# A two-layer decoder trunk: hidden blocks ranked earlier, a split cut in two, and the last pair of layer 1 by seven products

## The chip, the cores and the metric

The kernel runs on one core of one Trainium2 chip. The metric is the device time of one execution in microseconds. One profiled execution was taken of the kernel before; its trace has the start and duration of every instruction, what ended each idle time, and the issue and landing of every DMA.

## The reference

Two layers on 256 rows of 1024 numbers. Layer 0 mixes tokens by differential attention, layer 1 by block-sparse attention; each is followed by the MLP, around which this case turns:

```python
def squared_relu_mlp(h, w1, w2):
    return jnp.square(jax.nn.relu(h @ w1)) @ w2      # w1 1024x4096, w2 4096x1024

# for each layer i:
#   x = x + mixer_i(rmsnorm(x, attn_norm[i]))
#   x = x + squared_relu_mlp(rmsnorm(x, mlp_norm[i]), w_ff1[i], w_ff2[i])
# out = rmsnorm(x, final_norm)
```

## The kernel before

**Numbers in halves.** Every matmul operand is kept as two parts, `hi` (a rounded copy) and `lo` (what is left), and a product of two operands is three matmuls: hi·hi, lo·hi and hi·lo.

**Units.** The weights come in 96 units of 1 MB (some in pieces): `load` (L148) issues a unit's DMA on SP into one of four buffers `raw`, `need` calls for loads seven units ahead, and a split makes `hi` and `lo` of it: ACT copies (`hi`), DVE subtracts (`lo = raw − hi`), in `split_part` (L194 to L196). Layer 0 has units 0 to 47, layer 1 units 48 to 95. In layer 0, units 16 and 17 are the first two f1 pairs; from there on f1 unit of pair p is 14+2p and f2 unit of pair q is 19+2q, so that 41, 43, 45, 46, 47 are f2 of pairs 11, 12, 13, 14, 15 and 44 is f1 of pair 15. Layer 1's have 48 more (93, 94, 95: f2 of pairs 13, 14, 15).

There are three kinds of split. Most units go by `split_part`. The f1 units (`split_partly`, L184) do 3 of 8 chunks with ACT and an accumulating DMA of POOL. The f2 units go by `split_sums` (L165): besides `hi` and `lo` of the four 512-wide quarters, it makes three sums of quarters (`ts`, L177; then `raw` itself is changed by L179 and L180) with parts `thi` and `tlo`, which the seven products want. The `hi` of the whole raw (128x2048) waits for L180; only its upper half f=0 (128x1024) is complete after L179. L183 to L196 are where this happens.

**The MLP** (L684 to L922) goes over 16 pairs p of hidden blocks. `f1` (L694) puts a pair's activations into PSUM by 48 matmuls of 128x256, always in bank 0 (except p = 1); `hidden(p)` (L710) takes them out by relu and square on ACT (L717, L718), makes four sums on DVE (L722 to L724: `g`, 8 blocks in all) and splits them into `gh` and `gl`. `f2(p, ...)` (L732) multiplies by w2 with seven products in place of eight (as Strassen does for 2x2 blocks): seven PSUM banks M1 to M7 of 128x512, 3 matmuls each, 21 per pair. f2 runs two pairs behind f1. The last pair (15) goes by `direct` (L749), plain products of 24 matmuls that are put on top of the banks whose sums are ready or into a bank of its own, `rest`. `m_out` and `add` (L759 to L789) put the seven banks together into the rows xs: M1 is copied to `um` by ACT first, then DVE adds M6, M7, M5, M4, M3 in a chain, and M2.

**Order.** A tile scheduler with priorities orders each engine. Work has the rank of its place in the program; splits have a rank 150 places behind (`LATER`), and a block under `high_priority(offset=SOONER)` is ranked 100 places ahead. The PE order of attention (from L591) and the end of layer 1 (from L887) are written out by hand.

Of the kernel before, what the change touches and what calls it, by code (L numbers as in the profile page):

```python
# [9 lines left out]
F32 = mybir.dt.float32  # L10
F32R = mybir.dt.float32r
AF = mybir.ActivationFunctionType
# [3 lines left out]
D = 1024  # L16
T = 256
# [17 lines left out]
def kernel(  # L35
# [61 lines left out]
    for i in range(2):  # L97
# [33 lines left out]
        def f2_unit(j, a):  # L131
            U[i, "f2", j, a] = unit([P, 2, D], [
                ((slice(None),), f2[:, 4 * j + 2 * a: 4 * j + 2 * a + 2, :])])
            units[-1]["how"] = "sums" if (j, a) != (7, 1) else RING

# [29 lines left out]
    def split_sums(u):  # L165
# [15 lines left out]
        split_part(*(k.rearrange("p a b -> p (a b)") for k in (ts, thi[:, 1:], tlo[:, 1:])))  # L181
        split_part(*(k.rearrange("p a b -> p (a b)") for k in (raw, hi, lo)))

# [189 lines left out]
    def mixer(i, parts):  # L373
# [217 lines left out]
        with tc.manual_schedule(engines={mybir.EngineType.PE}):  # L591
# [34 lines left out]
            if i == 0:  # L626
                wo0(0)
                scores(6, 7)
                with tc.high_priority(offset=SOONER):
                    a3(5)  # L630
                wo0(1)
                a4(4)
                wo0(2, 3)
                a4(5)
# [49 lines left out]
    def mlp(i, parts):  # L684
# [4 lines left out]
        nc.vector.reciprocal(r2, v)  # L689
        NP = FF // P // 2  # L690
        Z = {}
        G = {}

        def f1(f, k0, k1):  # L694
# [12 lines left out]
            if f % 2 and k1 == KC:  # L707
                hidden(p)

        def hidden(p):  # L710
# [8 lines left out]
            n = 4  # L719
            if p < NP - 1:  # L720
                tt = nc.vector.tensor_tensor
                tt(g[:, 4], g[:, 1], g[:, 3], op=ALU.add)  # L722
                tt(g[:, 5:7], g[:, 1:5:3], g[:, 0:1].to_broadcast([P, 2, P]), op=ALU.subtract)
                tt(g[:, 7], g[:, 2], g[:, 6], op=ALU.subtract)  # L724
                n = 8
# [5 lines left out]

        def f2(p, ks):  # L732

            need(i, "f2", p // 2, p % 2)
            u = units[U[i, "f2", p // 2, p % 2]]
            gh, gl = G[p]
            for k in ks:
                g, names, w, n = SEVEN[k]
                if type(w) is tuple:
                    hi, lo = (u[q][:, w[0], w[1] * H:w[1] * H + H] for q in names)  # L740
                else:
                    hi, lo = (u[q][:, w] for q in names)
                if p == 0:
                    M[k] = bank(n, f"m{i}_{k}")
                for x, y in ((gh, hi), (gh, lo), (gl, hi)):
                    mm(M[k], x[:, g], y, start=p == 0 and x is gh and y is hi,  # L746
                       stop=p == LAST - 1 and x is gl, skip_group_check=True)

# [42 lines left out]
        def product(k):  # L791
            for p in range(LAST - 2, LAST):
                f2(p, (k,))
# [7 lines left out]
        for p in range(2, NP):  # L801
            f1(2 * p, 0, 8)
            f1(2 * p + 1, 0, 8)
            if p < LAST:
                f2(p - 2, SEVEN)
        if i == 0:
            parts3 = new_parts("e0")
            for p in (LAST - 2, LAST - 1):
                f2(p, (2, 7))
# [23 lines left out]
        else:  # L833
# [39 lines left out]

            for p in (LAST - 2, LAST - 1):
                f2(p, (5, 7))
# [4 lines left out]
            m_out(5)  # L880
            rest = bank(0, "rest")
            direct(1, H, D, rest, opens=True)
            add(1, 1, rest)
            product(4)
            direct(1, 0, H, M[4])
            m_out(4)
            with tc.manual_schedule():  # L887
                product(3)
                direct(0, H, D, M[3])
                y_sq(1, 512, 1024, 0)  # L890
# [6 lines left out]
                m_out(3)  # L897
                product(2)
                direct(0, 0, T, M[2][:, :T])
                scale_act(1, 512, 1024, r1)  # L900
# [8 lines left out]
                tail = bank(1, "tail")[:, :T]  # L909
                direct(0, T, H, tail, opens=True)  # L910
                y_add(0, 256, 512, tail)
# [48 lines left out]
```

## Time and profile before

| | us |
|---|---|
| three runs | 584.31, 584.61, 1980.6 |
| median | 584.61 |
| profiled execution, whole | 584.85 |
| its span (first to last instruction) | 583.0 |
| PE busy | 568.9 |
| DVE busy | 477.2 |
| ACT busy | 395.7 |

The span is what the trace shows; 1.85 us of the profiled execution lie around it. Engines are PE (matmul), PEld (its weight loads, which overlap), DVE, ACT, POOL and SP (which issues the loads of weights). PE's granted clock averaged 0.996 over the span. To read the tables: `out<-in` are the program's tiles, `x30` a count, and the idle time before an instruction is followed by what ended it.

### The profile page before, as it was taken

The page shows a single profiled execution, that of the slowest core. Times are in us where ns is not written, and L with a number is a line of the kernel's source. Part 1 is how long each engine was busy: PE and PEld are TensorE (multiplying, and loading weights), DVE is VectorE, ACT ScalarE, POOL GpSimd, SP SyncE. Part 2 cuts the span into 40 slices and gives each one's busy share as a digit, 9 for nine tenths or more (in the row PEclk, how much of TensorE's full clock was granted, in tenths as well). Part 3 has the DMA queues.
Part 4 walks back from the last instruction along what each step waited for, and adds up shares of the span by engine and source line. Part 5 has one row for each costly group of instructions (what it writes and reads, how often), then busy time and mean ns, then how long its engine had stood idle before and what let it go on. Part 6 is the DMA issues. An engine that isn't in the chain of part 4 may idle for free.

```text
span 583.0 us, 9723 instructions
## 1 busy us (share of the span) xinstructions
PE 568.9 (98%) x3784; PEld 509.0 (87%) x3784; DVE 477.2 (82%) x740; ACT 395.7 (68%) x632; POOL 89.2 (15%) x105
## 2 busy tenths in 40 slices
PE   8999999999999999999999999999999999999995
PEld 7889897899989899898789988878989989899874
DVE  4889578399999999988996664646999999998896
ACT  6776376297687786966675655645877686787653
POOL 6011001000011010100030760600001010010003
PEclk9999999999999999999999999999999999999998
DMA  9997444225878979876969445442467878979502
GB/s 304 291 324 237 153 137 144 74 73 194 233 233 247 246 211 247 235 215 217 268 189 264 146 146 158 140 136 70 142 179 241 235 213 249 257 209 293 154 0 73
DMA packets 94718, 113.36 MB, mean 194 GB/s; under 512 B 2480, under 2 KB 77520, under 8 KB 94672
## 3 DMA queue, kind: packets, MB, share of 16 engines
q1 hardware_dynamic: 84752, 103.03, 55.4%
q0 software_dynamic: 9760, 9.45, 10.9%
q8 instruction: 29, 0.48, 0.3%
q10 hardware_dynamic: 160, 0.27, 0.1%
q14 instruction: 17, 0.14, 0.1%
HBM read 111.69 MB, written 1.05 MB: 193 GB/s over the span
## 4 chain that ended last, share of the span: by engine, by line
PE 73%; DVE 14%; ACT 4%; DMA 4%; issue 3%; POOL 1%; SPq 0%; POOLq 0%; DVEq 0%; ACTq 0%
PE m L746 17%; PE f L704 8%; PE f L706 8%; PE f L705 8%; DVE lo L196 6%; PE z L396 4%; PE z L397 4%; PE z L398 4%; DMA raw<-in_w_ff_dram 3%; PE v L417 3%; PE v L419 3%; PE v L418 3%; ACT hi L195 2%; PE wo L552 2%; PE wo L554 2%
## 5 line engine op out<-in xcount | busy, mean ns | idle before, releaser
L195 ACT ACTIVATE hi<-raw 128x1024 fp32r<-128x1024 f32 (+3 forms) x136 | 173.7, 1294 | 105.5 <-DVE raw L180 53.6
L196 DVE TENSOR_TENSOR lo<-raw,hi 128x1024 fp32r<-128x1024 f32 (+3 forms) x134 | 203.4, 1533 | 44.3 <-ACT hi L195 42.5
L191 POOL DMA_DIRECT2D lo<-in_w_ff_dram x24 | 30.8, 1283 | 289.3 <-ACT lo L190 127.1
L704 PE MATMUL f<-xT_(0, 'm')_1444,hi 128*128 128x256 f32 x256 | 71.7, 281 | 0.0
L704 PE MATMUL f<-xT_(1, 'm')_4420,hi 128*128 128x256 f32 x256 | 71.6, 280 | 0.0
L705 PE MATMUL f<-xT_(0, 'm')_1444,hi 128*128 128x256 f32 x256 | 71.4, 280 | 0.0
L705 PE MATMUL f<-xT_(1, 'm')_4420,hi 128*128 128x256 f32 x256 | 71.4, 280 | 0.0
L706 PE MATMUL f<-xT_(1, 'm')_4420,lo 128*128 128x256 f32 x256 | 71.3, 279 | 0.0
L706 PE MATMUL f<-xT_(0, 'm')_1444,lo 128*128 128x256 f32 x256 | 71.3, 279 | 0.0
L704 PEld LDWEIGHTS f<-xT_(0, 'm')_1444,hi 128*128 128x128 f32 x256 | 48.0, 188 | 0.9 <-ACT g L717 0.3
L704 PEld LDWEIGHTS f<-xT_(1, 'm')_4420,hi 128*128 128x128 f32 x256 | 48.0, 188 | 0.8 <-ACT g L717 0.2
L705 PEld LDWEIGHTS f<-xT_(0, 'm')_1444,hi 128*128 128x128 f32 x256 | 47.9, 187 | 0.7
L705 PEld LDWEIGHTS f<-xT_(1, 'm')_4420,hi 128*128 128x128 f32 x256 | 47.9, 187 | 0.7
L706 PEld LDWEIGHTS f<-xT_(1, 'm')_4420,lo 128*128 128x128 f32 x256 | 48.1, 188 | 0.0
L706 PEld LDWEIGHTS f<-xT_(0, 'm')_1444,lo 128*128 128x128 f32 x256 | 48.1, 188 | 0.0
L746 PE MATMUL m<-hi,gl 128*128 128x512 f32 x120 | 47.4, 395 | 0.0
L746 PE MATMUL m<-hi,gh 128*128 128x512 f32 x120 | 47.3, 394 | 0.0
L746 PE MATMUL m<-lo,gh 128*128 128x512 f32 x120 | 47.3, 394 | 0.0
L195 ACT ACTIVATE gh<-g 128x1024 fp32r<-128x1024 f32 (+1 forms) x32 | 32.9, 1028 | 14.8 <-DVE g L724 14.4
L177 DVE TENSOR_TENSOR ts<-raw 128x1024 f32<-128x1024 f32 x30 | 36.6, 1220 | 4.6 <-DMA raw<-in_w_ff_dram 4.6
L746 PE MATMUL m<-thi,gl 128*128 128x512 f32 x90 | 35.8, 398 | 2.5 <-DVE gl L196 2.5
L196 DVE TENSOR_TENSOR gl<-g,gh 128x1024 fp32r<-128x1024 f32 (+1 forms) x32 | 37.8, 1186 | 0.0
(232 smaller groups left out, 1431.0 us busy)
## 6 DMA issues: line engine op xcount, KB each, us to landing
raw<-in_w_ff_dram SPq DMA_DIRECT2D x64, 1024.0 KB, 6.0
raw<-in_w_in_dram SPq DMA_DIRECT2D x30, 512.0 KB, 6.9
lo<-in_w_ff_dram POOLq DMA_DIRECT2D x24, 384.0 KB, 7.8
raw<-in_w_in_dram SPq DMA_DIRECT2D x8, 1024.0 KB, 6.6
raw<-in_w_out_dram SPq DMA_DIRECT2D x8, 1024.0 KB, 5.1
xs<-in_x_dram SPq DMA_DIRECT2D x2, 512.0 KB, 3.8
raw<-in_w_in_dram SPq DMA_DIRECT2D x4, 256.0 KB, 5.6
fg<-in_final_norm_dram SPq DMA_DIRECT2D x1, 512.0 KB, 4.6
```

The source lines that it names most:

```text
L177: tt(ts, r4[:, 1:2].to_broadcast([P, 2, h]), r4[:, 0:4:3], op=sub)
L191: nc.gpsimd.dma_start(lo[:, k], units[u]["pieces"][0][1][:, k], accum_op=ALU.add)
L195: nc.scalar.activation(h, r, AF.Copy)
L196: eng.tensor_tensor(l, r, h.bitcast(F32), op=ALU.subtract)
L396: mm(z, hi[:, s, kc], xh, start=s == 0 and kc == 0, stop=False, skip_group_check=True)
L397: mm(z, hi[:, s, kc], xl, start=False, stop=False, skip_group_check=True)
L398: mm(z, lo[:, s, kc], xh, start=False, stop=s == 1 and kc == KC - 1, skip_group_check=True)
L417: mm(o, xh, hi[:, c], start=kc == 0, stop=False)
L704: mm(z, hi[:, kc, c], xh, start=f % 2 == 0 and kc == 0, stop=False, skip_group_check=True)
L705: mm(z, hi[:, kc, c], xl, start=False, stop=False, skip_group_check=True)
L706: mm(z, lo[:, kc, c], xh, start=False, stop=f % 2 == 1 and kc == KC - 1, skip_group_check=True)
L746: mm(M[k], x[:, g], y, start=p == 0 and x is gh and y is hi, stop=p == LAST - 1 and x is gl, skip_group_check=True)
```

## The change

1. `hidden(p)` is called under `high_priority(offset=SOONER)`, 100 places up: relu, square, sums and gh/gl.
2. `split_sums` makes the `hi` of raw in two ACTIVATEs of 128x1024 (f = 0 and f = 1) with one DVE subtraction of 128x2048 behind them. The f = 0 half needs L179 but not L180.
3. In layer 1 the last pair goes by seven products too: its unit (95) is split "sums", `hidden` makes its sums, M1 to M7 close with pair 15 in place of 14, `direct` and the bank `rest` (and its `add`) are gone there. M2's matmuls of pair 15 come in two halves of 256, the second into a bank `tail`. Layer 0 keeps `direct` for pair 15.
4. In layer 0's attention the order on PE goes from `wo0(1); a4(4); wo0(2, 3)` to `wo0(1, 2); a4(4); wo0(3)`.

```diff
-            units[-1]["how"] = "sums" if (j, a) != (7, 1) else RING
+            units[-1]["how"] = RING if i == 0 and (j, a) == (7, 1) else "sums"
@@ split_sums
-        split_part(*(k.rearrange("p a b -> p (a b)") for k in (raw, hi, lo)))
+        for f in range(2):
+            nc.scalar.activation(hi[:, f], raw[:, f], AF.Copy)
+        nc.vector.tensor_tensor(lo, raw, hi.bitcast(F32), op=sub)
@@ attention, layer 0
-                wo0(1)
+                wo0(1, 2)
                 a4(4)
-                wo0(2, 3)
+                wo0(3)
@@ mlp
+        SUMS = NP - (i == 0)
             if f % 2 and k1 == KC:
-                hidden(p)
+                with tc.high_priority(offset=SOONER):
+                    hidden(p)
@@ hidden
-            if p < NP - 1:
+            if p < SUMS:
@@ f2
-                    mm(M[k], x[:, g], y, start=p == 0 and x is gh and y is hi,
-                       stop=p == LAST - 1 and x is gl, skip_group_check=True)
+                    mm(M[k][:, a:b] if o is None else o, x[:, g], y,
+                       start=(p == 0 or o is not None) and x is gh and y is hi,
+                       stop=p == SUMS - 1 and x is gl, skip_group_check=True)
@@ the last pairs of layer 1
             m_out(5)
-            rest = bank(0, "rest")
-            direct(1, H, D, rest, opens=True)
-            add(1, 1, rest)
             product(4)
-            direct(1, 0, H, M[4])
             m_out(4)
...
                 product(3)
-                direct(0, H, D, M[3])
...
-                product(2)
-                direct(0, 0, T, M[2][:, :T])
+                f2(SUMS - 2, (2,))
+                f2(SUMS - 1, (2,), 0, T)
...
-                direct(0, T, H, tail, opens=True)
+                f2(SUMS - 1, (2,), T, H, tail)
```

(`LAST` becomes `SUMS` in the loops over pairs: `p < SUMS`, `range(SUMS - 2, SUMS)`.)

The changed kernel's lines lie two further down from L183 to L600 or so, and four or five further down in the MLP: L196 is L198 there, L717 is L721, L722 to L724 are L726 to L728, L746 is L750. The `hi` of an f2 unit has line L183 and its `lo` L184.

**First place: DVE, towards the end of layer 0's MLP, around the sums (`ts`) of units 43 and 45.** The numbers in names are units (`raw41`) or layer and pair (`g0_12`). Before:

```order
L177 TENSOR_TENSOR ts43_2816<-raw43_2675 128x1024
L196 TENSOR_TENSOR lo41_2708<-raw41_2570,hi41_2707 128x2048
L722 TENSOR_TENSOR g0_12_2772<-g0_12_2772 128x128
L179 TENSOR_TENSOR raw43_2675<-raw43_2675,ts43_2816 128x512
L723 TENSOR_TENSOR g0_12_2772<-g0_12_2772 128x256
L196 TENSOR_TENSOR lo42_2783<-raw42_2600,hi42_2782 128x1280
L724 TENSOR_TENSOR g0_12_2772<-g0_12_2772 128x128
L196 TENSOR_TENSOR tlo43_2815<-raw43_2675,thi43_2814 128x512
L196 TENSOR_TENSOR tlo43_2815<-ts43_2816,thi43_2814 128x1024
L196 TENSOR_TENSOR gl0_12_2771<-g0_12_2772,gh0_12_2770 128x1024
L180 TENSOR_TENSOR raw43_2675<-raw43_2675 128x512
L177 TENSOR_TENSOR ts45_2922<-raw45_2780 128x1024
```

Of the change:

```order
L184 TENSOR_TENSOR lo41_2719<-raw41_2580,hi41_2718 128x2048
L198 TENSOR_TENSOR lo42_2795<-raw42_2610,hi42_2794 128x1280
L177 TENSOR_TENSOR ts43_2828<-raw43_2686 128x1024
L179 TENSOR_TENSOR raw43_2686<-raw43_2686,ts43_2828 128x512
L726 TENSOR_TENSOR g0_12_2784<-g0_12_2784 128x128
L727 TENSOR_TENSOR g0_12_2784<-g0_12_2784 128x256
L728 TENSOR_TENSOR g0_12_2784<-g0_12_2784 128x128
L177 TENSOR_TENSOR ts45_2935<-raw45_2792 128x1024
```

The sums of 43 and 45 moved up: `ts45` now stands closer behind `lo41`, the subtraction that reads raw41 last and so frees the buffer into which raw45 is loaded (the buffer of four units earlier); before there were nine instructions between them, now six, `gl0_12` and the parts of unit 43 among them.

**Second place: DVE and ACT, a little later, around `lo44` (f1 unit of pair 15) and the relu of pair 14.** DVE before:

```order
L177 TENSOR_TENSOR ts46_2997<-raw46_2810 128x1024
L196 TENSOR_TENSOR lo43_2813<-raw43_2675,hi43_2812 128x2048
L722 TENSOR_TENSOR g0_13_2877<-g0_13_2877 128x128
L179 TENSOR_TENSOR raw46_2810<-raw46_2810,ts46_2997 128x512
L723 TENSOR_TENSOR g0_13_2877<-g0_13_2877 128x256
L196 TENSOR_TENSOR lo44_2888<-raw44_2705,hi44_2887 128x1280
L724 TENSOR_TENSOR g0_13_2877<-g0_13_2877 128x128
L196 TENSOR_TENSOR tlo45_2921<-raw45_2780,thi45_2920 128x512
L196 TENSOR_TENSOR tlo45_2921<-ts45_2922,thi45_2920 128x1024
L196 TENSOR_TENSOR gl0_13_2876<-g0_13_2877,gh0_13_2875 128x1024
L180 TENSOR_TENSOR raw45_2780<-raw45_2780 128x512
L196 TENSOR_TENSOR lo45_2919<-raw45_2780,hi45_2918 128x2048
```

DVE of the change:

```order
L198 TENSOR_TENSOR lo44_2901<-raw44_2716,hi44_2900 128x1280
L726 TENSOR_TENSOR g0_13_2890<-g0_13_2890 128x128
L198 TENSOR_TENSOR tlo45_2934<-raw45_2792,thi45_2933 128x512
L727 TENSOR_TENSOR g0_13_2890<-g0_13_2890 128x256
L180 TENSOR_TENSOR raw45_2792<-raw45_2792 128x512
L728 TENSOR_TENSOR g0_13_2890<-g0_13_2890 128x128
L198 TENSOR_TENSOR tlo45_2934<-ts45_2935,thi45_2933 128x1024
L184 TENSOR_TENSOR lo45_2932<-raw45_2792,hi45_2931 128x2048
L198 TENSOR_TENSOR gl0_13_2889<-g0_13_2890,gh0_13_2888 128x1024
L179 TENSOR_TENSOR raw46_2822<-raw46_2822,ts46_3011 128x512
L726 TENSOR_TENSOR g0_14_2997<-g0_14_2997 128x128
```

The second step on raw46 (L179) stood ahead of `lo44`; it now stands behind `lo45` and `gl0_13`. On ACT in the same stretch, before:

```order
L195 ACTIVATE thi45_2920<-ts45_2922 128x1024
L195 ACTIVATE gh0_13_2875<-g0_13_2877 128x1024
L195 ACTIVATE hi45_2918<-raw45_2780 128x2048
L717 ACTIVATE g0_14_2983<-f0_14_2932 128x512
L195 ACTIVATE thi46_2995<-raw46_2810 128x512
L718 ACTIVATE g0_14_2983<-g0_14_2983 128x512
L195 ACTIVATE thi46_2995<-ts46_2997 128x1024
L195 ACTIVATE hi46_2993<-raw46_2810 128x2048
L195 ACTIVATE gh0_14_2981<-g0_14_2983 128x1024
L195 ACTIVATE hi47_3030<-raw47_2885 128x2048
```

ACT of the change:

```order
L183 ACTIVATE hi45_2931<-raw45_2792 128x1024
L197 ACTIVATE gh0_13_2888<-g0_13_2890 128x1024
L183 ACTIVATE hi46_3007<-raw46_2822 128x1024
L721 ACTIVATE g0_14_2997<-f0_14_2946 128x512
L197 ACTIVATE hi47_3045<-raw47_2898 128x2048
L722 ACTIVATE g0_14_2997<-g0_14_2997 128x512
L197 ACTIVATE thi46_3009<-raw46_2822 128x512
L197 ACTIVATE thi46_3009<-ts46_3011 128x1024
L197 ACTIVATE gh0_14_2995<-g0_14_2997 128x1024
L183 ACTIVATE hi46_3007<-raw46_2822 128x1024
```

The relu of pair 14 (`g0_14<-f0_14`) has the upper half of hi46, which needs L179 of unit 46, ahead of it; before it had hi45 ahead of it. The whole hi47 went ahead of the square of pair 14, which before had only one piece of thi46 ahead.

**Third place: PE, end of layer 1's MLP, where M1 is closed.** Before (`m1_1` is M1 of layer 1):

```order
L746 MATMUL m1_1_4720<-hi94_5964,gh1_14_5954 128x512
L746 MATMUL m1_1_4720<-lo94_5965,gh1_14_5954 128x512
L746 MATMUL m1_1_4720<-hi94_5964,gl1_14_5955 128x512
L746 MATMUL m1_6_4724<-hi93_5891,gh1_13_5851 128x512
L746 MATMUL m1_6_4724<-lo93_5892,gh1_13_5851 128x512
L746 MATMUL m1_6_4724<-hi93_5891,gl1_13_5852 128x512
L746 MATMUL m1_6_4724<-hi94_5964,gh1_14_5954 128x512
L746 MATMUL m1_6_4724<-lo94_5965,gh1_14_5954 128x512
L746 MATMUL m1_6_4724<-hi94_5964,gl1_14_5955 128x512
L756 MATMUL rest_6098<-hi95_5999,gh1_15_6052 128x512
```

Of the change:

```order
L750 MATMUL m1_1_4737<-hi94_5993,gh1_14_5983 128x512
L750 MATMUL m1_1_4737<-lo94_5994,gh1_14_5983 128x512
L750 MATMUL m1_1_4737<-hi94_5993,gl1_14_5984 128x512
L750 MATMUL m1_1_4737<-hi95_6029,gh1_15_6093 128x512
L750 MATMUL m1_6_4741<-hi94_5993,gh1_14_5983 128x512
L750 MATMUL m1_6_4741<-lo94_5994,gh1_14_5983 128x512
L750 MATMUL m1_1_4737<-lo95_6030,gh1_15_6093 128x512
L750 MATMUL m1_1_4737<-hi95_6029,gl1_15_6094 128x512
L750 MATMUL m1_6_4741<-hi94_5993,gl1_14_5984 128x512
```

M1 was closed by pair 14; now it is closed by pair 15 (hi95 and lo95 with gh1_15 and gl1_15), behind products 5 and 7 of pairs 14 and 15.

## Rows read from the trace of the kernel before

**Rows 1.** The page, part 1: busy time (share of the span) and instructions.
```profile
PE 568.9 (98%) x3784; PEld 509.0 (87%) x3784; DVE 477.2 (82%) x740; ACT 395.7 (68%) x632; POOL 89.2 (15%) x105
```
**Rows 2.** Windows, layer 0's MLP: length; busy PE, PEld, DVE, ACT, POOL; clock, DMA, GB/s.
```profile
140.00:263.00 123.00, 123.00 (x809) 111.93 (x808) 116.16 (x129) 91.93 (x104) 15.43 (x12) 1.00 0.82 229
```
**Rows 3.** PE's waits by releaser: us in all, times, longest.
```profile
PE m L746 <- DVE gl L196: 2.5, 2, 1.3
```
**Rows 4.** Timeline of PE, layer 1's end: start, us, instruction, idle time before it.
```profile
559.13 0.40 PE L746 MATMUL m<-thi,gh 128*128 128x512 f32 x1
...
562.37 0.50 PE L746 MATMUL m<-thi,gl 128*128 128x512 f32 x1 [1.26 <-DVE gl L196]
...
564.57 0.40 PE L746 MATMUL m<-hi,gl 128*128 128x512 f32 x1
...
566.21 0.39 PE L756 MATMUL rest<-hi,gh 128*128 128x512 f32 x1
...
575.88 0.28 PE L756 MATMUL tail<-hi,gl 128*128 128x256 f32 x1
```
**Rows 5.** Timelines of ACT and DVE, layer 1's end.
```profile
565.01 0.60 ACT L772 ACTIVATE um<-m 128x512 f32<-128x512 f32 x1 [1.60 <-PE m L746]
...
569.92 0.75 DVE L761 SCALAR_TENSOR_TENSOR xs<-rest,r,xs 128x512 f32<-128x512 f32 x1
570.61 0.69 DVE L783 TENSOR_TENSOR um<-m,um 128x512 f32<-128x512 f32 x1
571.34 1.32 DVE L761 SCALAR_TENSOR_TENSOR xs<-um,r,xs 128x512 f32<-128x512 f32 x1
...
578.77 0.48 DVE L920 SCALAR_TENSOR_TENSOR xg<-xs,vt,fg 128x256 f32<-128x256 f32 x1
```
**Rows 6.** Groups of instructions by shape: count, busy us, mean ns, idle before.
```profile
L195 ACT ACTIVATE hi<-raw 128x1024 fp32r<-128x1024 f32 x68 | 70.0, 1054 | 37.2 <-issue 14.1 <-PE v L419 9.7 <-PE z L397 7.8
L177 DVE TENSOR_TENSOR ts<-raw 128x1024 f32<-128x1024 f32 x30 | 36.6, 1220 | 4.6 <-DMA raw<-in_w_ff_dram 4.6
L179 DVE TENSOR_TENSOR raw<-raw,ts 128x512 f32<-128x512 f32 x30 | 20.7, 689 | 0.6
L723 DVE TENSOR_TENSOR g<-g 128x256 f32<-128x256 f32 x30 | 12.7, 422 | 0.5
L724 DVE TENSOR_TENSOR g<-g 128x128 f32<-128x128 f32 x30 | 8.7, 289 | 0.5
```
**Rows 7.** The page, part 6, then tile raw from 140 to 263: issue to landing, us.
```profile
raw<-in_w_ff_dram SPq DMA_DIRECT2D x64, 1024.0 KB, 6.0
...
DMA to landing us min/median/max: 5.4/7.9/10.7
```
**Rows 8.** Timeline of DVE, layer 0's MLP from pair 13 on.
```profile
254.55 1.23 DVE L177 TENSOR_TENSOR ts<-raw 128x1024 f32<-128x1024 f32 x1 [1.66 <-DMA raw<-in_w_ff_dram]
...
261.65 1.48 DVE L196 TENSOR_TENSOR lo<-raw,hi 128x1280 fp32r<-128x1280 f32 x1
...
282.63 0.69 DVE L196 TENSOR_TENSOR gl<-g,gh 128x512 fp32r<-128x512 f32 x1
...
287.96 0.75 DVE L761 SCALAR_TENSOR_TENSOR xs<-m,r,xs 128x512 f32<-128x512 f32 x1
```
**Rows 9.** Timelines of PE and ACT, end of layer 0's MLP.
```profile
269.30 0.39 PE L704 MATMUL f<-xT_(0, 'm')_1444,hi 128*128 128x256 f32 x1
...
275.06 0.40 PE L746 MATMUL m<-thi,gh 128*128 128x512 f32 x1
...
284.01 0.39 PE L756 MATMUL m<-hi,gl 128*128 128x512 f32 x1
...
288.74 0.63 ACT L312 ACTIVATE junk_e<-xs 128x512 f32<-128x512 f32 x1 [5.42 <-DVE xs L761]
...
292.83 0.45 ACT L289 ACTIVATE xT_(1, 'a')_3203<-xtp_(1, 'a')_0_0_3204,gT 128x256 fp32r<-128x256 f32 x1
...
293.33 0.50 PE L417 MATMUL v<-hi,xT_(1, 'a')_3203 128*128 128x512 f32 x1 [0.37 <-ACT xT_(1, 'a')_3203 L289]
```

More of the change, by code (lines that the diff above doesn't have):

```diff
@@ L730, in mlp, with f2 @@
         LAST = NP - 1
-        def f2(p, ks):
+        def f2(p, ks, a=0, b=H, o=None):
             need(i, "f2", p // 2, p % 2)
@@ L739, in f2 @@
                 if type(w) is tuple:
-                    hi, lo = (u[q][:, w[0], w[1] * H:w[1] * H + H] for q in names)
+                    hi, lo = (u[q][:, w[0], w[1] * H + a:w[1] * H + b] for q in names)
                 else:
-                    hi, lo = (u[q][:, w] for q in names)
+                    hi, lo = (u[q][:, w, a:b] for q in names)
                 if p == 0:
@@ L791, in product @@
         def product(k):
-            for p in range(LAST - 2, LAST):
+            for p in range(SUMS - 2, SUMS):
                 f2(p, (k,))
@@ L803, in mlp @@
             f1(2 * p + 1, 0, 8)
-            if p < LAST:
+            if p < SUMS:
                 f2(p - 2, SEVEN)
@@ L807, in mlp @@
             parts3 = new_parts("e0")
-            for p in (LAST - 2, LAST - 1):
+            for p in (SUMS - 2, SUMS - 1):
                 f2(p, (2, 7))
@@ L872, in scale_act @@
                 nc.scalar.activation(xg[:, t, a:b], xg[:, t, a:b], AF.Copy, scale=r)
-            for p in (LAST - 2, LAST - 1):
+            for p in (SUMS - 2, SUMS - 1):
                 f2(p, (5, 7))
```

## The prediction

> **What bounds the kernel now.** I read the busy times first: PE works in 568.9 of 583.0 us, DVE in 477.2, ACT in 395.7 [rows 1]. Then a window over layer 0's MLP, which says how: from 140 to 263 PE is busy in all 123.00 us at a granted clock of 1.00, while DVE is idle for 123.00 − 116.16 = 6.84 us and ACT for 31 [rows 2]. So in the MLP's steady part PE sets the pace, and an earlier relu or hi gains nothing there. What the change can gain lies where PE waits, and the waits of PE show what that is in the MLP: `f2` waits twice for `gl`, 2.5 us in all [rows 3]. The one in layer 1 is at 562.37 [rows 4]: the matmul before it started some 1.26 + .23 us earlier, so PE lost about 1.5 us there, and as much at the same place in layer 0.
>
> Last I read both timelines at the end of layer 1. M1's last matmul runs from 564.57 to 564.97 [rows 4]; ACT starts to copy M1 at 565.01, and from there DVE's chain of adds and norm pieces runs close to the end at 583.0 [rows 5]. PE is done at 575.88 + .28 = 576.2 [rows 4], ahead of the chain in each bank. So the last 583.0 − 565.0 = 18.0 us hang on when M1 is complete and on DVE and ACT behind it, not on how many matmuls PE has left.
>
> **The end of layer 1.** The last f1 matmul ends where the first f2 matmul of pair 13 starts, 559.13. PE's pitch in f2 is (566.21 − 564.57) / 7 = .234 us a matmul [rows 4]. By the third order M1's last matmul is now one of pair 15: ahead of it stand pair 13 (21), products 5 and 7 of pairs 14 and 15 (12), six of M1 less the last (5) and two of M6, 40 in all. With no wait of PE on the way it starts at 559.13 + 40 × .234 = 568.5 and ends at 568.9, against 564.97: +3.9. This already gives back the 1.5 us of the gl wait, which I take as gone (gl14 now stands well ahead of its use). Off comes the add of `rest` on DVE, a pitch of 570.61 − 569.92 = .69 (its whole duration is .75) [rows 5]; I take .85, its duration and a gap of .1 ahead of it, so 3.9 − .85. Sum of this part: **+3.0 us**. The three matmuls less (66 to 63, .7 us) count nothing, since PE's end is not what is waited for.
>
> The sums that pair 15 now needs cost DVE 1.22 (ts) + 2 × .69 (L179, L180) + 1.00 (g) [rows 6], and some 1.8 for tlo and the longer gl, near 6 us, and ACT some 2. They fall in the 21 matmuls of pair 13 (4.9 us) and the time ahead, in which DVE had stood waiting. I cost them at nothing; lo95 has to be there by the 40th matmul, 568.5, and by my count it is there 0.3 to 1 us earlier. If that cover is gone, each us of lateness is a us at the end.
>
> Two hi of 1024 cost 2 × 1.05 [rows 6] in place of one of 2048 near 1.91, .2 us more of ACT per unit, thirty times: nothing, since ACT has 31 us idle in the window.
>
> **The end of layer 0.** This is where order decides. The first order puts ts45 closer behind `lo41`. lo41 frees the buffer that raw45 is loaded into; between them DVE now has 1.48 (lo42) [rows 8] + 1.22 + .69 + .29 + .42 + .29 [rows 6] = 4.4 us of work. A load of 1 MB takes 6.0 us in the median of 64; from 140 to 263 the least is 5.4 and the median 7.9 [rows 7] (that one mixes f2's loads with f1's, which run beside POOL's). So DVE now waits for raw at ts41 and at ts45: load less 4.4 each, and at ts37, by the same order, load less 5.6. In before it waited at ts45 as well, 1.66 us [rows 8]. I take 6.0, the median of all, since f2's loads lie below f1's: 1.6 + 1.6 + .4, and .5 for waits on ACT that stay: 4.1, where 6.84 were idle. So `lo44` ends E = 263.13 − 2.7 = 260.4 (before 261.65 + 1.48 = 263.13 [rows 8]). Written with the load L: E = 242.4 + 3L, from 258.8 (L = 5.4, where ts37 waits no more) to 266.1 (7.9).
>
> From E on I added pitches along the second orders. L179 of unit 46 is done at E + 7.0, hi46's upper half at E + 8.0, the relu of pair 14 at E + 8.5. f1 of pair 15 needs bank 0 from it and started at 269.30 [rows 9]; 268.9 is just in time. The square of pair 14 stands behind the whole hi47 (1.8 us) and ends at E + 10.9, DVE idle for 3.9 us meanwhile; then the sums, unit 46's and 47's lo, three more, and gl15 is done at E + 23.5 = 283.9. PE wants it in the third `direct` matmul. That ran at 284.01; without the gl14 wait PE would be there at 269.30 + 5.76 (275.06 − 269.30) + 32 × .234 = 282.5 [rows 9]. So the 1.5 us that the earlier gl14 gives are **given back at gl15**: PE runs the third direct near 284.0 as before. DVE's five adds behind it end at E + 28.5 = 288.9 (before 287.96 + .75 = 288.71 [rows 8]), and ACT then has two junks and four hi ahead of the transposed x (xT) where it had three: 5.0 us in place of 292.83 − 288.74 = 4.1 [rows 9]. xT comes at 293.9 in place of 292.83, and layer 1's v, which waited for xT [rows 9], starts **1.1 us** later.
>
> Layer 1's MLP repeats this order with everything shifted; f1(15) is again just covered: 0. The move of wo0(2) ahead of a4(4) reorders PE work of the same size beside waits of .5 that are there in any order: 0.
>
> **Sum.** 583.0 + 3.0 + 1.1 = 587.1 in the span, with 1.85 around it **589.0 us**, against 584.85 of the profiled execution; the median of the runs is .24 lower.
>
> **The rivals.** First, *the loads are not waited for* (they land by 5.4 or sooner). Then E ≤ 258.8, gl15 is in time, and layer 0 gains: xT .4 earlier at 5.4, 587.5 us; with all 1.5 us kept, 583.0 + 3.0 − 1.5 + 1.85 = 586.4; with PE's other small MLP waits gone too, 585.3. For it: loads of f2 that run beside no other land near the least, 5.4 [rows 7]. Against it: 1.66 us of waiting at ts45 in before [rows 8]. Beside it stands a rule of the Trainium skill, page "DMA: Bandwidth & Descriptors", section "Anatomy of one DMA — SWDGE (gpsimd) path": a DMA takes about 2.0 us plus its bytes by 436 thousand per us. By that rule a load takes 4.4 us (an estimate; the fit is for DMAs issued from GpSimd, and SP issues these), no ts waits, and the time is 586.4. The trace does not agree: 5.4 at the least, 6.0 in the median [rows 7].
>
> Second, *the loads bind*: L = 7.9, E = 266.1, the relu of pair 14 is 5.3 us late for f1(15) in layer 0, xT 6.8 late, f1(15) 5.3 late in layer 1 as well: 583.0 + 3.0 + 6.8 + 5.3 + 1.85 = 600.0. From E = 260.8 on each us of E counts twice. L = 7.0 gives 594.6. For it: 7.9 as the window's median, three loads at a time near the MLP's end; against it: the f2 loads of the steady part.
>
> Third, *faster*: PE's end decides, not the chain. Then three matmuls (.7) and both gl waits (2 × 1.5) go: 583.0 − 3.7 + 1.85 = 581.2. This wants the chain behind M1 shorter by 3.0 us for no change and by 6.8 for the full gain. In it I see one thing that could shrink, an add of 1.32 where others took .75 [rows 5], .6 us. Little speaks for it. That nothing changes at all is the same rival half way, 583 to 585.
>
> **Chances.** My forecast, 587.5 to 592, .54; the first rival, 585 to 587.5, .20; faster or no change below 585, .10; loads binding, above 592, .16, of which half lies above 594.5. So 585.0 to 594.5 holds .82; the low end is the first rival's best, the high end is L = 7.0. What a measurement of this kernel tells from no change is about 2%: below 572.9 or above 596.3. No case but a mishap reaches the first (.01); L above some 7.2 gives the second (.06); within 2%: .93.
>
> **What would show it.** Right: M1's last matmul ending some 41 matmuls after the last f1, ACT's copy of it right behind, some 17.2 us before the end, PE done well before; no wait of PE for gl of pair 14 and in its place one for gl15 at layer 0's end; ts on DVE idle for DMA more often than 4.6 us in all; xT of layer 1 later by about one. Wrong: a chain behind M1 shorter than 17 us, PE waiting in f1(15) for the relu, ts without DMA waits, or lo95 late for M1, with PE waiting right ahead of its end. The load time is the weakest number: E moves by 3 us with each us of it.

## The result, and the profile after

The changed kernel takes 589.08 us in the median (588.67 to 589.45, four runs), the kernel before, run along with it, 585.09 (one of its four runs took 1980.6 us; the ratio leaves that run out). The ratio is 1.0062, with a 95% interval of 1.0047 to 1.0077: slower by 0.6%, 4.0 us between the medians. The forecast was 589.0, with 585.0 to 594.5 around it. The profiled execution spans 587.4 us against 583.0.

The page of the kernel after, part 1 (busy us, share of the span, instructions), answers to [rows 1]:

```profile
PE 569.0 (97%) x3778; PEld 509.4 (87%) x3778; DVE 479.4 (82%) x747; ACT 405.2 (69%) x665; POOL 88.2 (15%) x105
```

PE has as much busy time as before (569.0 and 568.9 us), though 6 instructions fewer stand on it (the work of three matmuls of 512; some are 256 wide): the 4.4 us are idle time. PE's waits (releaser, us in all, times, longest) say where a part of it is, beside [rows 3]:

```profile
PE v L419 <- ACT xT_(1, 'a')_3218 L291: 1.8, 1, 1.8
...
PE m L761 <- DVE gl L198: 1.0, 1, 1.0
```

The wait of f2 for gl of pair 14 (2.5 us in two places before) is gone. In its place `direct` waits 1.0 us for gl of pair 15 in layer 0, and layer 1's v waits 1.8 us for xT, where it had waited .37 [rows 9].

The same in order of time, PE after, which answers to [rows 4, 9] (start, us, instruction, idle time before it):

```profile
269.72 0.28 PE L707 MATMUL f<-xT_(0, 'm')_1444,hi 128*128 128x256 f32 x1
...
284.02 0.51 PE L761 MATMUL m<-hi,gl 128*128 128x512 f32 x1 [1.04 <-DVE gl L198]
...
294.92 0.50 PE L419 MATMUL v<-hi,xT_(1, 'a')_3218 128*128 128x512 f32 x1 [1.85 <-ACT xT_(1, 'a')_3218 L291]
...
555.01 0.28 PE L707 MATMUL f<-xT_(1, 'm')_4435,hi 128*128 128x256 f32 x1
...
570.02 0.63 PE L750 MATMUL m<-hi,gl 128*128 128x512 f32 x2
...
575.28 0.28 PE L750 MATMUL tail<-thi,gl 128*128 128x256 f32 x1
```

And the end of layer 1 on ACT and DVE after, which answers to [rows 5]:

```profile
570.45 0.60 ACT L777 ACTIVATE um<-m 128x512 f32<-128x512 f32 x1 [4.02 <-PE m L750]
...
571.09 0.75 DVE L766 SCALAR_TENSOR_TENSOR xs<-um,r,xs 128x512 f32<-128x512 f32 x1 [1.58 <-ACT um L777]
...
575.78 1.32 DVE L766 SCALAR_TENSOR_TENSOR xs<-um,r,xs 128x512 f32<-128x512 f32 x1
...
583.18 0.48 DVE L920 SCALAR_TENSOR_TENSOR xg<-xs,vt,fg 128x256 f32<-128x256 f32 x1
```

M1 is complete at 570.4 (565.0 before). PE has its last work done at 575.6, .6 us sooner than the kernel before, and the kernel ends 4.4 us later. That is the case in a sentence: less matmul work, and the bank that starts the last chain closed later.

Four marks cut the span into stretches that can be compared among all kernels of this study: the first f1 matmul of pair 15 in layer 0, the same in layer 1, ACT's copy of layer 1's M1, and the end. All are read from the profiled executions; the runs named e1 to e9 are those of the next section. In the kernel before, the second mark, which the rows ahead of the prediction do not show, is this row:

```profile
553.43 0.33 PE L704 MATMUL f<-xT_(1, 'm')_4420,hi 128*128 128x256 f32 x1
```

| us | to f1(15), layer 0 | to f1(15), layer 1 | to the copy of M1 | to the end | span |
|---|---|---|---|---|---|
| before | 269.30 | 284.13 | 11.58 | 17.99 | 583.0 |
| after | 269.72 | 285.29 | 15.44 | 16.95 | 587.4 |
| e1, no seven products | 270.26 | 285.62 | 10.02 | 18.40 | 584.3 |
| e2, seven products alone | 269.07 | 284.04 | 16.98 | 17.01 | 587.1 |
| e3, M1 later | 269.41 | 283.75 | 12.82 | 18.12 | 584.1 |
| e4, e1 and x transposed earlier | 269.55 | 284.81 | 10.02 | 18.52 | 582.9 |
| e5, e1 and hi47 in halves | 269.07 | 287.77 | 10.13 | 18.73 | 585.7 |
| e6, e4 and hi47 in halves | 268.95 | 285.89 | 10.12 | 18.74 | 583.7 |
| e7, rank alone | 269.04 | 284.57 | 11.63 | 17.96 | 583.2 |
| e8, halves in layer 1 alone | 269.01 | 284.12 | 10.02 | 18.35 | 581.5 |
| e9, halves of two units | 270.03 | 284.13 | 9.79 | 18.05 | 582.0 |

The first column differs by up to 1.3 us, also among kernels that are alike there (before, e2, e3, e7, e8 and e9 from 269.01 to 270.03); the difference is there from the first loads and the first attention heads. Of the 4.4 us between before and after it holds .4, layer 0's end and layer 1 up to pair 15 hold 1.2, and the end of layer 1 3.86 − 1.04 = 2.8.

### The profile page after: what moved, and what is told of

It reads as the page before. It is cut to its first block, busy times and chain, and to the rows that moved or that the text cites. A ratio compares the mean times of both kernels' runs of the same rounds, so it can differ in the third digit from the quotient of the medians.

```text
span 587.4 us, 9763 instructions
## 1 busy us (share of the span) xinstructions
PE 569.0 (97%) x3778; PEld 509.4 (87%) x3778; DVE 479.4 (82%) x747; ACT 405.2 (69%) x665; POOL 88.2 (15%) x105
## 4 chain that ended last, share of the span: by engine, by line
PE 84%; DVE 7%; ACT 4%; DMA 2%; issue 1%; POOL 1%; POOLq 0%; DVEq 0%; ACTq 0%
PE m L750 23%; PE f L707 10%; PE f L709 10%; PE f L708 10%; PE z L398 4%; PE z L399 4%; PE z L400 4%; PE wo L556 2%; PE wo L554 2%; PE v L419 2%; PE wo L555 2%; PE v L420 2%; PE v L421 2%; ACT hi L197 2%; DVE lo L198 2%; PE s L438 2%
## 5 line engine op out<-in xcount | busy, mean ns | idle before, releaser
L198 DVE TENSOR_TENSOR lo<-raw,hi 128x1024 fp32r<-128x1024 f32 (+3 forms) x103 | 132.7, 1307 | 31.7 <-ACT hi L197 31.6
L197 ACT ACTIVATE hi<-raw 128x1024 fp32r<-128x1024 f32 (+3 forms) x105 | 114.2, 1110 | 51.8 <-PE wo L556 15.3
L183 ACT ACTIVATE hi<-raw 128x1024 fp32r<-128x1024 f32 x62 | 65.2, 1052 | 29.7 <-DVE raw L180 16.3
L184 DVE TENSOR_TENSOR lo<-raw,hi 128x2048 fp32r<-128x2048 f32 x31 | 70.8, 2285 | 2.1 <-ACT hi L183 2.1
L707 PE MATMUL f<-xT_(1, 'm')_4435,hi 128*128 128x256 f32 x256 | 71.6, 280 | 0.0
L708 PE MATMUL f<-xT_(1, 'm')_4435,hi 128*128 128x256 f32 x256 | 71.4, 280 | 0.0
L709 PE MATMUL f<-xT_(1, 'm')_4435,lo 128*128 128x256 f32 x256 | 71.3, 279 | 0.0
L750 PE MATMUL m<-hi,gl 128*128 128x512 f32 x124 | 48.8, 395 | 0.0
L750 PE MATMUL m<-hi,gh 128*128 128x512 f32 x124 | 48.7, 394 | 0.0
L750 PE MATMUL m<-lo,gh 128*128 128x512 f32 x124 | 48.7, 394 | 0.0
L707 PEld LDWEIGHTS f<-xT_(1, 'm')_4435,hi 128*128 128x128 f32 x256 | 48.0, 188 | 0.7
L708 PEld LDWEIGHTS f<-xT_(1, 'm')_4435,hi 128*128 128x128 f32 x256 | 47.9, 187 | 0.7
L709 PEld LDWEIGHTS f<-xT_(1, 'm')_4435,lo 128*128 128x128 f32 x256 | 48.1, 188 | 0.0
```

Source lines behind the costliest of these rows:

```text
L183: nc.scalar.activation(hi[:, f], raw[:, f], AF.Copy)
L184: nc.vector.tensor_tensor(lo, raw, hi.bitcast(F32), op=sub)
L197: nc.scalar.activation(h, r, AF.Copy)
L198: eng.tensor_tensor(l, r, h.bitcast(F32), op=ALU.subtract)
L707: mm(z, hi[:, kc, c], xh, start=f % 2 == 0 and kc == 0, stop=False, skip_group_check=True)
L708: mm(z, hi[:, kc, c], xl, start=False, stop=False, skip_group_check=True)
```

## The experiments

Of the parts of the change, two are told apart by the programs alone. With the rank of `hidden` raised and nothing else, the built program has the same instructions in the same order on every engine as the kernel before. And without the seven products, the splits in halves alone give the same orders as with rank and the attention's wo0 added, but for the one transpose of `a4(4)`. So what the places on DVE and ACT showed ahead of the prediction is the work of the halves.

**e7: the rank alone.**

```diff
-                hidden(p)
+                with tc.high_priority(offset=SOONER):
+                    hidden(p)
```

> The kernel before with the rank of hidden raised by 100 and nothing else. The built program has the same instructions in the same order on each engine as the kernel before. Theory: ratio 1.000 within 0.001, and what it differs by is what two runs of one program differ by here. Rival (rank decides the order): there is no way for it to show.

Measured: ratio 1.0001 (0.9989 to 1.0013). Two builds of one program differ by that much here, and their profiles by .2 us in span. The title's first part does nothing.

**e1: the change without the seven products.** The last pair's unit in layer 1 is split as in layer 0, `direct` and `rest` stay:

```diff
-        SUMS = NP - (i == 0)
+        SUMS = NP - 1
...
             m_out(5)
+            rest = bank(0, "rest")
+            direct(1, H, D, rest, opens=True)
+            add(1, 1, rest)
             product(4)
+            direct(1, 0, H, M[4])
```

> The change without the seven products for layer 1's last pair (that pair plain again, with its bank rest). Theory (two separate places: layer 0's end costs 1.1 us, layer 1's end costs 3.0 because M1 closes later): M1 closes with pair 14 again, 18 matmuls after the last f1, and the gl wait of 1.5 us that stood before it is gone since the order of the halves brings gl14 earlier. Span 583.0 + 1.1 - 1.5 = 582.6, so 0.4 us below the kernel before (ratio 0.999, 0.998 to 1.001). Rival (the slower time comes from the new order of splits in both layers, the seven products being cheap): still 587 or more, 2.5 us above before, with waits of PE in layer 1's MLP.

Measured: ratio 1.0005 (0.9993 to 1.0016), span 584.3. The end of layer 1 went as the theory said: 10.02 us from pair 15's f1 to the copy of M1 in place of 11.58, and no wait for gl14. The rival had 587. But between the two marks of pair 15's f1 it loses 1.5 us against before (285.62 and 284.13), not 1.1, and not where I had them:

```profile
270.26 0.28 PE L707 MATMUL f<-xT_(0, 'm')_1444,hi 128*128 128x256 f32 x1
...
283.54 0.51 PE L761 MATMUL m<-hi,gl 128*128 128x512 f32 x1
...
294.44 0.59 PE L419 MATMUL v<-hi,xT_(1, 'a')_3218 128*128 128x512 f32 x1 [1.85 <-ACT xT_(1, 'a')_3218 L291]
```

Up to v it takes 294.44 − 270.26 = 24.18 us, only .15 more than before (24.03), while the kernel after takes 25.20, although the instructions of layer 0 and their order are the same in both. PE came to pair 15's f1 .54 us later here and DVE had gl15 ready .48 us sooner, so the third `direct` matmul has no listed wait. The rest is lost behind v, and for that the profile has a reason that I had not reckoned with. Windows of 2 us behind v's wait for xT (length, busy PE, PEld, DVE, ACT and POOL, granted clock, DMA share, GB/s), first e1, then the kernel after:

```profile
294.00:296.00 2.00, 1.56 (x4) 1.28 (x5) 2.00 (x5) 2.00 (x6) 0.88 (x2) 0.68 0.21 54
296.00:298.00 2.00, 2.00 (x6) 1.56 (x6) 2.00 (x4) 2.00 (x6) 1.16 (x3) 0.50 1.15 330
298.00:300.00 2.00, 2.00 (x17) 1.92 (x16) 1.59 (x3) 1.16 (x4) 0.00 (x0) 0.97 0.61 145
```

```profile
294.00:296.00 2.00, 1.08 (x5) 0.91 (x6) 2.00 (x4) 2.00 (x4) 0.49 (x1) 1.00 0.07 22
296.00:298.00 2.00, 2.00 (x14) 1.78 (x13) 2.00 (x5) 2.00 (x6) 1.55 (x4) 1.00 0.98 294
```

In e1 the granted clock fell to 0.50, the lower of its two levels (1.2 GHz), for about 3.5 us right after PE's idle time of 1.85 us. In that time v's matmuls start .43 us apart:

```profile
296.75 0.63 PE L419 MATMUL v<-hi,xT_(1, 'a')_3218 128*128 128x512 f32 x1
297.18 0.63 PE L420 MATMUL v<-lo,xT_(1, 'a')_3218 128*128 128x512 f32 x1
```

From v to pair 15's f1 in layer 1 it takes 555.88 − 294.44 = 261.44 us, against 260.09 in the kernel after, where the clock did not fall though the wait is the same. So 1.35 of the 1.5 us are the clock's. e1's other ten executions have no profile. Their mean granted clocks lie between .993 and .998, as they would if the clock fell in some of them, but those of the kernel before (.994 to .999) spread nearly as far, so how often it fell was not seen.

**e2: the seven products alone**, on the kernel before, with whole hi and the old attention order:

```diff
-            units[-1]["how"] = "sums" if (j, a) != (7, 1) else RING
+            units[-1]["how"] = RING if i == 0 and (j, a) == (7, 1) else "sums"
...
+        SUMS = NP - (i == 0)
...
-            direct(1, H, D, rest, opens=True)
```

> The kernel before with only the seven products for layer 1's last pair; splits of hi whole, attention order as before. Theory (M1 closing late): nothing moves up to 559; M1 closes 41 matmuls after the last f1, at 568.9, or about 1 us later if lo95, which now follows one undivided hi of 2048, is late; then 17.0 us to the end. Span 586.0 to 587.1, 3.0 to 4.0 us above before (ratio 1.005 to 1.007). Rival (three matmuls fewer shorten the end, and the loss lies in layer 0): 0 to 0.7 us below before.

Measured: ratio 1.0070 (1.0058 to 1.0082), span 587.1, at the upper end of what the theory gave. All of it lies at the end of layer 1: 16.98 us to the copy of M1, 5.4 more than before, and 17.01 from there, 1.0 less. PE on the way, and the copy:

```profile
566.70 0.50 PE L747 MATMUL m<-tlo,gh 128*128 128x512 f32 x1 [0.77 <-DVE tlo L196]
```

```profile
570.09 0.60 ACT L774 ACTIVATE um<-m 128x512 f32<-128x512 f32 x1 [3.15 <-PE m L747]
```

With whole hi the sums of pair 15 come late (a wait of .77 for tlo), as was feared for lo95. In the kernel after, with halves, no such wait is in the trace. A wait for gl of pair 14 is not in layer 1 here either, though hi is whole: the 21 matmuls of pair 13 now stand ahead of the first use of gl14. The rival, that three matmuls fewer shorten the end, is out.

**e3: M1 later, with nothing added.** On the kernel before, product 6 goes ahead of product 1:

```diff
-            for k in (1, 6):
+            for k in (6, 1):
                 product(k)
-                m_out(k)
+            m_out(1)
+            m_out(6)
             m_out(7)
```

> The kernel before with product 6 put ahead of product 1 at layer 1's end: the same 66 matmuls, M1's last one six places later on PE, nothing else in another order. Theory (the end hangs on M1's closing and the chain of DVE behind it): 6 x 0.234 = 1.4 us later, span 584.4, ratio 1.0024. Rival (the amount of work on PE or on DVE after the last f1 sets the end): no change, since neither has more to do.

Measured: ratio 1.0022 (1.0014 to 1.0031), 1.3 us; 12.82 us to the copy of M1 in place of 11.58, and 18.12 behind it in place of 17.99.

```profile
565.98 0.60 ACT L772 ACTIVATE um<-m 128x512 f32<-128x512 f32 x1 [2.99 <-PE m L746]
```

Six matmuls moved, no work added, and the end moved with the closing of M1. This run shows the mechanism alone.

**e4: x transposed earlier**, on e1. The call for the first half of layer 1's transposed x goes ahead of `direct(0, H, D, M[3])`:

```diff
             product(3)
+            boundary((1, "a"), 0, 2 * KC)
             direct(0, H, D, M[3])
             m_out(3)
             rest = bank(0, "rest")
             direct(1, H, D, rest, opens=True)
-            boundary((1, "a"), 0, 2 * KC)
```

> The first run of this list (no seven products) with the transposes of layer 1's first half of x put 12 matmuls earlier in the program, so that ACT takes them (xT) behind one of the four hi of 1024 that stood ahead. Theory (layer 0's end is priced by the wait of v for xT, 1.85 us in the trace of the change): that wait goes, some may come back where the second half of x is late; 1.2 to 1.9 us below the first run, so 581 or 1.6 to 2.3 below before in the span (ratio to before 0.996 to 0.9975). Rival (v waits only because PE ran ahead; the second half of x or the pieces of hi for layer 1 are late next by the same amount): no gain against the first run.

Measured: ratio 0.9988 (0.9973 to 1.0003), 0.17% below e1, about 1.0 us; 1.2 was the least I had expected. v's wait for xT is gone and two smaller ones are there; the last row below is the larger:

```profile
284.01 0.50 PE L761 MATMUL m<-hi,gl 128*128 128x512 f32 x1 [1.21 <-DVE gl L198]
...
294.69 0.50 PE L419 MATMUL v<-hi,xT_(1, 'a')_3203 128*128 128x512 f32 x1
...
295.88 0.50 PE L421 MATMUL v<-hi,xT_(1, 'a')_3203 128*128 128x512 f32 x1 [0.47 <-DVE xT_(1, 'a')_3203 L292]
```

The wait for xT was priced right, but half of it comes back a few matmuls on, at the second chunk of x, whose low part stands behind a lo of layer 1's weights on DVE. The clock stayed at 1.00. So part of the 1.0 us may be the clock that fell in e1 and not the wait; against the kernel after, where it did not fall, e4 is .5 us shorter between the two marks of f1(15) (284.81 and 285.29).

**e5: the last unit's hi in two halves** (`PIECE` is 1024), on e1:

```diff
-            units[-1]["how"] = "sums" if (j, a) != (7, 1) else RING
+            units[-1]["how"] = "sums" if (j, a) != (7, 1) else PIECE
```

> The first run of this list (e1, no seven products) with one thing more: the last pair's unit in each layer (47, 95), whose hi was one ACTIVATE of 128x2048, is split in two pieces of 1024. In layer 0 the square of pair 14 then stands behind one half of hi47. Theory (gl15 is late because the square of pair 14 waits for all of hi47, and this lateness gives back what the earlier gl14 won): square and all behind it .95 us earlier, PE's wait for gl15 of 1.0 us nearly gone (0.1), add, junk and xT .9 earlier: 0.9 us below e1, ratio to before 0.998 to 1.000. Rival (gl15 is late because DVE has lo46, lo47, lo48 and half of lo49 ahead of it, 8 us whatever ACT does): no gain against e1, wait of 1.0 stays.

Measured: ratio 1.0017 (1.0000 to 1.0034). The theory fell: no gain, and the wait for gl15 stays.

```profile
283.59 0.50 PE L761 MATMUL m<-hi,gl 128*128 128x512 f32 x1 [1.27 <-DVE gl L198]
```

(The 1.0 us that the expectation names is the wait of the kernel after; in e1's own profile it is not listed.) The square of pair 14 does come earlier, DVE's idle time ahead of pair 14's sums falls from 3.98 to 3.13 us, and it is lost again on the way to gl15:

```profile
262.75 2.28 DVE L184 TENSOR_TENSOR lo<-raw,hi 128x2048 fp32r<-128x2048 f32 x1
...
269.90 0.29 DVE L726 TENSOR_TENSOR g<-g 128x128 f32<-128x128 f32 x1 [3.13 <-ACT g L722]
...
271.36 0.69 DVE L198 TENSOR_TENSOR tlo<-raw,thi 128x512 fp32r<-128x512 f32 x1 [0.39 <-ACT thi L197]
...
282.85 0.68 DVE L198 TENSOR_TENSOR gl<-g,gh 128x512 fp32r<-128x512 f32 x1
```

Counted from the start of lo45, the first row, the sums of pair 14 start at 7.15 us in place of 7.99 in the kernel after, and the subtraction that makes gl15 at 20.10 in place of 20.15 (its rows stand in the next section): of .84 us won .05 are left. From the first sum to gl15 DVE takes 282.85 − 269.90 = 12.95 us, and 283.28 − 271.12 = 12.16 after. Half of the difference, .39, is a wait for thi46, which on ACT now stands behind the second half of hi47. The other half goes in the instructions themselves: DVE has the sums, tlo46 and L180 in another order there, and lo47 in two pieces. So the square alone does not set gl15, and the edit moved more than the square. Whether another order of the same work would bring gl15 sooner was not tried. This profile, too, has the clock at 0.50 behind v's wait, from 296 to 298, and an f1 that waits for a relu in layer 1, where a ts waited for its load:

```profile
546.11 0.39 PE L707 MATMUL f<-xT_(1, 'm')_4437,hi 128*128 128x256 f32 x1 [0.58 <-ACT g L721]
```

```profile
538.10 1.22 DVE L177 TENSOR_TENSOR ts<-raw 128x1024 f32<-128x1024 f32 x1 [2.19 <-DMA raw<-in_w_ff_dram]
```

That may be the prediction's second rival, binding loads, in small. It is not shown: e7, whose program is the kernel before, has two such waits of .3 us at f1(15).

**e6: e4 and e5 together.**

> e4 (no seven products, transposes of x earlier) and e5 (last unit's hi in two) together. Theory: the two gains lie one behind the other on the same chain and add: 0.9 us below e4, span near 582.0 with a start like that of e4, ratio to before 0.996 to 0.998; PE's waits at layer 0's end 1.0 us in all in place of 2.1. Rival (PE at the end of layer 1 or the clock takes it back): no more than e4's gain, 0.9985 to 0.999.

Measured: ratio 0.9985 (0.9969 to 1.0002), no more than e4. The gains do not add, since e5 has none. The clock stayed at 1.00 here behind v's wait, so it is not the clock that hides a gain of e5.

**e8: halves in layer 1 alone**, the rest as before:

```diff
-        split_part(*(k.rearrange("p a b -> p (a b)") for k in (raw, hi, lo)))
+        if u >= 48:
+            for f in range(2):
+                nc.scalar.activation(hi[:, f], raw[:, f], AF.Copy)
+            nc.vector.tensor_tensor(lo, raw, hi.bitcast(F32), op=sub)
+        else:
+            split_part(*(k.rearrange("p a b -> p (a b)") for k in (raw, hi, lo)))
```

> The kernel before with the hi of f2 units in two halves in layer 1 alone (units 48 and up); layer 0, the attention and the plain last pair as before. Theory (in layer 0 the halves win the gl14 wait and lose it again at gl15 and at xT; in layer 1, where nothing waits at that place, they keep it): layer 0 as before with its gl wait near 1.2 and v's .4, layer 1 without the gl wait, M1 closed some 10 us after the start of pair 15's f1 in place of 11.6, then 18.0 to 18.4 to the end. Span 583.0 - 1.6 + 0.4 = 581.8, ratio 0.997 to 0.999. Rival (the halves' loop of loads costs as much in layer 1 as it wins): 0.999 to 1.002, with f1 of pair 15 waiting for the relu of pair 14.

Measured: ratio 0.9965 (0.9952 to 0.9979), span 581.5. All four stretches are as expected: layer 0 as before (284.12), 10.02 to the copy of M1, 18.35 behind it.

```profile
563.15 0.60 ACT L779 ACTIVATE um<-m 128x512 f32<-128x512 f32 x1 [2.24 <-PE m L752]
```

e8 and e1 differ by the halves in layer 0 alone (and one transpose of `a4(4)`). Their ratios, 0.9965 and 1.0005, lie .4% apart, some 2.3 us, give or take 1 by the intervals. So halves in layer 0 cost more there than the 1.1 us of the forecast. The 1.35 us of the clock would nearly make up the difference if most executions of e1 lost them, which no run shows.

**e9: halves for units 93 and 94 alone.**

```diff
-        if u >= 48:
+        if u in (93, 94):
```

> The kernel before with hi in two halves for units 93 and 94 alone (f2 of pairs 13 and 14 of layer 1). In before DVE waited 1.98 us for hi93, which came after L180, and .65 for hi94. Theory (the gl14 wait comes from the DVE queue's waits for these two hi, not from the places of ts, which stay here): gl14 1 to 2 us earlier, PE's wait for it 0 to 0.5 in place of 1.3 with no more waits for loads; span 581.8 to 582.5, ratio 0.998 to 0.999. Rival (gl14 comes earlier only because ts and the loads move up): wait and time as before, 1.000.

Measured: ratio 0.9967 (0.9954 to 0.9979), the same gain as e8 within the intervals. PE waits once for gl, in layer 0, and no more in layer 1:

```profile
PE m L752 <- DVE gl L201: 1.2, 1, 1.2
```

DVE's waits for hi93 and hi94 are gone as well. So the wait for gl14 came from two hi that were copied late and whole, and DVE's waits for them (with the halves the scheduler also put L180 of unit 93 one place up on DVE); that ts and the loads move up is not needed for the gain. e8 and e9 are both faster than the kernel before and the kernel after.

## Why the prediction was right, step by step

**What bounds the kernel: right.** PE busy time did not move, and 4.0 of the 4.4 us lie at the two places that the prediction named. The matmuls that were saved bought nothing (e2, e3).

**The end of layer 1, +3.0: measured +2.8.** Counted from the first f1 matmul of pair 15, M1's copy came 3.86 us later (forecast 3.9), and the rest of the chain took 16.95 us in place of 17.99 (forecast 17.1). The assumption that gl14's wait goes was right, though in layer 1 the new order on PE alone does it (e2). The one that lo95 comes in time was right as well: its subtraction ended at 567.22 + 2.29 = 569.51, and M1's matmul with it started near 569.8 (the trace has it as the second of two from 569.55 on), .3 us later (forecast 0.3 to 1). No wait is in the trace. The cover was as thin as said; without the halves it was gone (e2, .77 us). e3 shows the mechanism by itself.

```profile
567.22 2.29 DVE L184 TENSOR_TENSOR lo<-raw,hi 128x2048 fp32r<-128x2048 f32 x1
```

**The end of layer 0, +1.1: measured +1.2 in its stretch, in part by luck.** The times came out close, but not all by the forecast's way. DVE and ACT after, around `lo44` and gl15:

```profile
245.71 1.22 DVE L177 TENSOR_TENSOR ts<-raw 128x1024 f32<-128x1024 f32 x1
250.08 1.23 DVE L177 TENSOR_TENSOR ts<-raw 128x1024 f32<-128x1024 f32 x1 [1.44 <-DMA raw<-in_w_ff_dram]
...
258.64 1.49 DVE L198 TENSOR_TENSOR lo<-raw,hi 128x1280 fp32r<-128x1280 f32 x1
...
263.13 2.28 DVE L184 TENSOR_TENSOR lo<-raw,hi 128x2048 fp32r<-128x2048 f32 x1
...
271.12 0.29 DVE L726 TENSOR_TENSOR g<-g 128x128 f32<-128x128 f32 x1 [3.98 <-ACT g L722]
...
283.28 0.68 DVE L198 TENSOR_TENSOR gl<-g,gh 128x512 fp32r<-128x512 f32 x1
...
289.24 0.63 ACT L314 ACTIVATE junk_e<-xs 128x512 f32<-128x512 f32 x1 [8.52 <-DVE xs L766]
...
294.41 0.45 ACT L291 ACTIVATE xT_(1, 'a')_3218<-xtp_(1, 'a')_0_0_3219,gT 128x256 fp32r<-128x256 f32 x1
```

`lo44` ended at 258.64 + 1.49 = 260.13 (forecast 260.4). The forecast took the 2.7 us off DVE's idle time. Windows from 140 to the end of `lo44`, after and then before, with the columns of [rows 2], show something else:

```profile
140.00:260.13 120.13, 120.13 (x783) 108.99 (x782) 113.59 (x128) 96.42 (x117) 15.43 (x12) 1.00 0.81 230
```

```profile
140.00:263.13 123.13, 123.13 (x810) 112.06 (x809) 116.29 (x130) 91.93 (x104) 15.43 (x12) 1.00 0.82 229
```

DVE was idle for 120.13 − 113.59 = 6.54 us, and before for 6.84: .3 less, where the forecast had 2.7 less. Its work ahead of `lo44` is less, by 116.29 − 113.59 = 2.7 us. 1.4 of these are the step on raw46 (L179, .69) and two sums of pair 13 (.42 and .29), which stood ahead of `lo44` and now stand behind it; where the rest went was not traced. That two numbers of 2.7 stand for different things is luck. The waits of ts for loads were 1.77, 1.52 and 1.44 at units 37, 41 and 45 (forecast .4, 1.6, 1.6).

From `lo44` on the steps held. gl15 was done at 283.96 (forecast 283.9), the third direct matmul ran at 284.02 as before, with a wait of 1.04 (forecast: as before, with 1.4), xT came at 294.41 (293.9), and v 1.59 us later than before. .42 of this was there at pair 15's f1 and came from the kernel's start, which leaves 1.2 (forecast 1.1). But this subtraction is not firm: in e1, with the same program in layer 0, it leaves .15. From the start of lo45 on DVE to v it is 31.8 us in both profiles (294.92 − 263.13, and 294.44 − 262.64 in e1), so v came by DVE's chain and not by the time at which PE came to f1(15). From the start of the span, v is 1.59 us later in the kernel after and 1.11 in e1. The forecast of 1.1 lies within these counts, .15 to 1.6, and is not confirmed more closely than that.

The load time, called the weakest number, held at units 41 and 45 by the wait that it gives; at unit 37 and as a median over all loads it did not (6.8 us after in place of 6.0):

```profile
raw<-in_w_ff_dram SPq DMA_DIRECT2D x64, 1024.0 KB, 6.8
```

**"Given back at gl15": the size right, its cause not borne out.** The prediction named the square of pair 14 behind the whole hi47 as what makes gl15 late. e5 took half of hi47 out of its way; the square came .84 us sooner behind lo45, and gl15 .05. The square's place is then not the whole cause, for the order of ACT and DVE behind it took the gain back. Which piece of that work could be put off was not tried.

**Layer 1 in between, 0: right.** From v to pair 15's f1 it takes 555.01 − 294.92 = 260.09 us after and 553.43 − 293.33 = 260.10 before. f1(15) waits for no relu in the profile after.

**The move of wo0, 0: right.** Pair 15's f1 in layer 0 came .42 us later than before, and the kernel was .63 late already at its first z matmul with lo (8.50 against 7.87), far ahead of the attention's end. That the rank does nothing at all (e7) was not seen ahead; the prediction priced the orders as a whole, so it did no harm.

**The rivals.** That the end of PE decides (581.2) is out by e2 and e3. That layer 0 keeps its gains (585.3 to 587.5) did not happen, for ts did wait for loads. Binding loads (592 and more) did not happen either; the .58 us in e5 may be a trace of it. What was not among the rivals is that the clock can fall behind PE's wait for xT.

## What to carry to other kernels

Where the last stage is a chain on one engine that starts from one accumulator, the date at which that accumulator closes sets the end, and a cheaper algorithm that closes it later is slower: count matmuls up to its last one, not in all. A stall that an earlier operand removes is a gain only if the next operand on the same path is not late by as much; look for the second wait before counting the first. And take a change of several parts apart: here one part did nothing, one cost 3 to 4 us, and a third, kept to the two units where it pays (e9), is worth 0.3%. A forecast that comes out may still have summed the wrong thing: lo44 came when it was due, by less work and not by less waiting.

## What the runs showed of the hardware that I had not expected

The granted clock fell from 1.00 to 0.50 for some 3.5 us after PE had been idle for 1.85 us at v's wait for xT, in the profiles of e1 and e5 and not in that of the kernel after, which has the same wait. PE then started its matmuls of 512 every .43 us in place of .23. In the kernels with waits of .5 us or less at that place (before, e2 to e4, e6 to e9) it stayed at 1.00, and so it did around the waits of 1.04 and 1.27 us for gl15 in the kernel after and e5 (windows of 2 us from 282 to 288). What decides between the two was not settled.
